# A pad of 64 bytes behind the weight buffers of a two-layer transformer kernel

## The chip, the cores and the metric

The kernel runs on one core of one Trainium2 chip. The time is that of one execution on the device in microseconds (us); three executions are given, and their median counts. One more execution was taken with the hardware profiler, and all rows shown here come from it.

## What is computed

The reference is a small hybrid transformer in fp32: 512 tokens, width 1024, two layers. Cut to its core:

```python
for layer in range(2):
    if layer == 0:    # attention with a forget gate, 16 heads of 64
        x = x + fox_mixer(rmsnorm(x, fox_norm), w_fox_in, b_fox_f, w_fox_out)
    else:             # latent attention, 16 heads, 128 + 64 rotary
        k_nope, k_rope, v = mla_shared_kv(x, kv_in_norm, w_dkv, kv_norm, w_uk, w_uv, cos, sin)
        x = x + mla_mixer(rmsnorm(x, mla_norm), w_dq, q_norm, w_uq, w_mla_out, k_nope, k_rope, v, cos, sin)
    x = x + conv_ffn(rmsnorm(x, ffn_norm[layer]), w_ffn_in[layer], conv_w[layer], conv_b[layer], w_ffn_out[layer])
return rmsnorm(x, final_norm)
```

## The kernel before

Activations are kept transposed: 128 features on the partitions, the 512 tokens along the row. Every fp32 number that goes through TensorE is split into a high and a low part, and a product is made of three matmuls: high weight by high activation, high by low, low by high. `mm3` (L82) issues them as L84, L85 and L86. For each matmul TensorE reads two operands from SBUF: the stationary one (here called the weight read, the first operand, LDWEIGHTS in the trace, 128 columns of 4 bytes on each partition) and the moving one (mostly 512 columns of 4 bytes). In `mm3` the stationary operand is a piece of a weight matrix and the moving one an activation. In two places it is the other way round: `mm_v` (L416 to L418) and `proj_v` (L687 to L689) hold the activation and stream the weights. The transposes of the attention (L227) hold a tile of the probabilities and stream the identity matrix `idf`.

`load_w` (L88) brings every weight: SyncE issues the DMA into a tile `raw`, ScalarE makes the high part `whi` (L105), VectorE or GpSimd the low part `wlo` (L106). There are three `raw` buffers and two each of `whi` and `wlo`, 4096 bytes a partition each.

The stages follow each other: the V projection (`mm_v`), then 16 heads of the first attention with the Q and K projections and part of the output projection filled in between, the first feed-forward block, the latent attention in the same manner, the second feed-forward block, and a tail that normalises and writes out in two halves. Order is program order on each engine.

Where a buffer lies within a partition follows from the order of the pools and the sizes of their tiles: pools lie one behind the other in the order in which they are opened, a tag's buffers one behind the other in the order in which tags first appear, and sizes are rounded up to 32 bytes. So there lie, in this order: `sp` (small things), `cp` (the residual `xT`, `idf`, `ones_r`, the scratch tiles `r2` and `R`), `wp` (`raw`, `whi`, `wlo`), `bp` (three buffers `big` of 32768 bytes, which hold the split activations), and the pool of the stage (`fx`, `ffn0`, `ml`, `ffn1`), with the probabilities, the split queries and keys, the third part of the feed-forward activations `act2` and so on. The buffers of `wp` come to 3 x 4096 + 2 x 4096 + 2 x 4096 = 28672 bytes, which is 112 x 256. All sizes in `cp`, `bp` and the stage pools add up to multiples of 256 too; where a small tile would break this it is made larger than what is used, as in

```python
        bfb = T(fp, [P, 64], F32, "bfb", 1)[:, :FH]
        rl = T(p_pool, [P, 16], F32, "rl", 2)[:, :NT]
            conv = T(fp, [P, 192], F32, "conv", 1)[:, :KF * 8]...
```

So every operand that TensorE reads in this kernel starts at the same place modulo 256 as every other one, with few exceptions. The one that matters here is the first third of `mm_v`, whose weight tile has two halves of 272 columns: the second, `w[0][:, 1, :]`, starts 272 x 4 = 1088 = 4 x 256 + 64 bytes into its buffer. The order of that stage is, for each of four pairs `kp`: 12 matmuls on the first half (kk = 0), then 12 on the second (kk = 1).

Of the kernel before, what the change touches and what calls it, by code (L numbers as in the profile page):

```python
# [7 lines left out]
F32 = mybir.dt.float32  # L8
# [7 lines left out]
P = 128  # L16
# [30 lines left out]
def tile_kernel(ctx, tc, xT_d, gains_d, bf_d, const_d, conv_d, wv_d, wq_d, wk_d, wfo_d,  # L47
                wdq_d, wdkv_d, wuqn_d, wuqr_d, wuk_d, wuv_d, wmo_d, wfi_d, wfu_d, out_d):
    nc = tc.nc
    v, a, g, pe = nc.vector, nc.scalar, nc.gpsimd, nc.tensor  # L50
# [4 lines left out]
    wp = ctx.enter_context(tc.tile_pool(name="wp", bufs=2))  # L55
# [2 lines left out]
    dp = ctx.enter_context(tc.tile_pool(name="dp", bufs=1, space=DRAM))  # L58

    cnt = [0]  # L60

    def T(pool, shape, dt, tag, bufs=None):
        cnt[0] += 1
        kw = {} if bufs is None else {"bufs": bufs}
        return pool.tile(shape, dt, tag=tag, name=f"{tag}_{cnt[0]}", **kw)
# [13 lines left out]
    def f(ap):  # L79
        return ap.bitcast(F32)  # L80
# [7 lines left out]
    def load_w(src, shape, gain=None, eng=None, into=None, pieces=1):  # L88

        n = 1  # L90
        for s in shape[1:]:
            n *= s
        raw = T(wp, [P, 1024], F32, "raw", 3)[:, :n]
        cuts = [slice(i * n // pieces, (i + 1) * n // pieces) for i in range(pieces)]
        for c in cuts:
            nc.sync.dma_start(raw[:, c], src[:, c])
        if gain is not None:
            k, c = gain
            r3 = raw.rearrange("p (k c) -> p k c", c=n // k)
            g.tensor_tensor(out=r3, in0=r3, in1=c.unsqueeze(2).to_broadcast([P, k, n // k]), op=ALU.mult)  # L100
        if into is None:
            into = T(wp, [P, 1024], F32R, "whi", 2), T(wp, [P, 1024], F32R, "wlo", 2)
        hi, lo = (t[:, :n] for t in into)
        for c in cuts:
            a.copy(hi[:, c], raw[:, c])  # L105
            (eng or v).tensor_tensor(out=lo[:, c], in0=raw[:, c], in1=f(hi[:, c]), op=ALU.subtract)  # L106
        names = " ".join(f"d{i}" for i in range(len(shape) - 1))
        kw = {f"d{i}": shape[i + 1] for i in range(len(shape) - 1)}
        pat = f"p ({names}) -> p {names}"
        return hi.rearrange(pat, **kw), lo.rearrange(pat, **kw)  # L110
# [168 lines left out]
    def ffn(layer, xs, squares, gbase):  # L279
        with tc.tile_pool(name=f"ffn{layer}", bufs=1, reuse_waits="tile") as fp:  # L280
# [21 lines left out]
            for j in range(KF):  # L302
                for b in range(2):
                    wh, wl = load_w(wfi_d[layer, j, b], [P, KD, P])
                    pt = acc()
                    for k in range(KD):
                        mm3(pt, (wh[:, k, :], wl[:, k, :]), parts(xs, k), k == 0, k == KD - 1)
                    rstd.after(lambda R, j=j, b=b, pt=pt: evacuate(j, b, pt, R))
# [3 lines left out]
            def load(d, c):  # L312
                k0, kn = chunks[c]
                return load_w(wfu_d[layer, d, :, k0 * P:(k0 + kn) * P], [P, kn, P])
# [76 lines left out]
    with tc.tile_pool(name="fx", bufs=1, reuse_waits="tile") as fp:  # L391
# [7 lines left out]
        def load_v(c, kp):  # L399
            if c == 2:  # L400
                nc.sync.dma_start(xT[:, 2 * kp, :], xT_d[2 * kp])
            w = load_w(wv_d[c][kp], [P, 2, VCH[c + 1] - VCH[c]], pieces=2 if (c, kp) == (2, 0) else 1)
            if c == 2:
                nc.sync.dma_start(xT[:, 2 * kp + 1, :], xT_d[2 * kp + 1])
            return w
# [475 lines left out]
```

## Time and profile before

| | us |
|---|---|
| three executions | 1430.11, 1433.37, 1434.18 |
| median | 1433.37 |
| the profiled execution | 1429.15 |
| its span, from the first to the last instruction | 1427.1 |
| TensorE busy | 1384.2 (97% of the span) |
| VectorE busy | 902.9 (63%) |
| ScalarE busy | 636.5 (45%) |
| GpSimd busy | 310.6 (22%) |
| mean granted TensorE clock | 0.983 of full speed |

The profiled execution lies 2.05 us above its span and 4.22 us (0.29%) below the median of the three. A matmul's recorded time runs into the next one's, since they are pipelined; what a matmul costs in a stream is the distance from its start to the start of the next.

### The profile page before, as it was taken

Reading aid. Unit: us, or ns where it says so; the run is one execution under the profiler, and the core shown is the slowest. Engines: PE = TensorE matmul, PEld = TensorE weight load, DVE = VectorE, ACT = ScalarE, POOL = GpSimd, SP = SyncE. Lnnn points to the kernel's source line nnn. Section 1 sums busy time; section 2 is a strip of 40 time slices with the busy share of each in tenths; the row PEclk is TensorE's granted clock in tenths of the full one; section 3 lists DMA queues with packets and bytes.
Section 4 is the critical chain, followed back from the end, with each engine's and each line's share of the span. In section 5 each row is a group of like instructions: output and inputs, shape, how many; then the busy total and the mean of one; then the engine's idle time right before and its main releaser. Section 6 shows DMA issues by size and latency. Waiting matters only on the chain.

```text
span 1427.1 us, 17362 instructions
## 1 busy us (share of the span) xinstructions
PE 1384.2 (97%) x6594; PEld 1162.8 (81%) x6594; DVE 902.9 (63%) x1495; ACT 636.5 (45%) x1103; POOL 310.6 (22%) x228
## 2 busy tenths in 40 slices
PE   7999999899999999999799999999999999999997
PEld 7888887788888888888678888888888888888886
DVE  6667786677776744445876666665557777774333
ACT  5588884254444432223454555543225444442111
POOL 4333322400000002154533333321310000000222
PEclk9999999999999999999999999999999999999998
DMA  5321112222323233332111111212232323323331
GB/s 178 102 76 61 51 51 68 89 96 96 103 90 104 89 92 97 106 105 80 50 49 48 59 49 52 61 54 89 89 104 89 104 91 101 98 94 93 96 97 69
DMA packets 41251, 120.22 MB, mean 84 GB/s; under 512 B 5552, under 2 KB 9952, under 8 KB 41168
## 3 DMA queue, kind: packets, MB, share of 16 engines
q1 hardware_dynamic: 39184, 117.00, 25.8%
q0 software_dynamic: 1840, 2.09, 0.6%
q8 instruction: 51, 0.84, 0.2%
q14 instruction: 32, 0.26, 0.1%
q10 hardware_dynamic: 144, 0.03, 0.0%
HBM read 116.74 MB, written 2.36 MB: 83 GB/s over the span
## 4 chain that ended last, share of the span: by engine, by line
PE 85%; DVE 8%; ACT 3%; issue 3%; DMA 1%; POOL 1%; SPq 0%; DVEq 0%; POOLq 0%; ACTq 0%
PE acc L84 24%; PE acc L86 23%; PE acc L85 23%; PE att L208 6%; DVE r L637 2%; PE acc L556 1%; PE att L227 1%; PE acc L709 1%; DVE r L638 1%; DVE ptl L231 1%; DVE big L190 1%; ACT whi L105 1%; DVE tr L667 1%; PE att L84 1%; PE att L86 1%
## 5 line engine op out<-in xcount | busy, mean ns | idle before, releaser
L86 PE MATMUL acc<-big,wlo 128*128 128x512 f32 (+1 forms) x1504 | 584.9, 389 | 7.5 <-POOL wlo L106 3.9
L84 PE MATMUL acc<-big,whi 128*128 128x512 f32 (+1 forms) x1504 | 587.5, 391 | 3.1 <-ACT big L189 2.2
L85 PE MATMUL acc<-big,whi 128*128 128x512 f32 (+1 forms) x1504 | 584.5, 389 | 0.3 <-DVE big L190 0.3
L105 ACT CAST whi<-raw 128x1024 fp32r<-128x1024 f32 (+4 forms) x243 | 229.3, 944 | 427.7 <-PE acc L85 267.5
L86 PEld LDWEIGHTS acc<-big,wlo 128*128 128x128 f32 x1504 | 283.8, 189 | 67.9 <-POOL wlo L106 5.8
L84 PEld LDWEIGHTS acc<-big,whi 128*128 128x128 f32 x1504 | 283.7, 189 | 61.0 <-ACT big L189 2.8
L85 PEld LDWEIGHTS acc<-big,whi 128*128 128x128 f32 x1504 | 283.8, 189 | 58.2 <-DVE big L190 0.6
L106 DVE TENSOR_TENSOR wlo<-raw,whi 128x1024 fp32r<-128x1024 f32 (+3 forms) x179 | 236.2, 1320 | 141.0 <-ACT whi L105 138.3
L142 POOL TENSOR_TENSOR r<-xT 128x512 f32<-128x512 f32 x28 | 31.4, 1124 | 735.9 <-DVE xT L254 414.5
L106 POOL TENSOR_TENSOR wlo<-raw,whi 128x768 fp32r<-128x768 f32 (+3 forms) x64 | 111.8, 1749 | 223.1 <-ACT whi L105 197.3
L294 DVE SCALAR_TENSOR_TENSOR c<-u,conv,c 128x510 f32<-128x510 f32 (+1 forms) x176 | 131.1, 747 | 3.5 <-ACT c L292 0.6
L289 DVE TENSOR_TENSOR u<-acc,R 128x512 f32<-128x512 f32 x88 | 60.3, 687 | 76.3 <-PE acc L86 76.3
L213 ACT ACTIVATE e<-e,nm 128x128 f32<-128x128 f32 (+3 forms) x128 | 71.3, 557 | 43.1 <-DVE nm L211 42.1
L146 POOL TENSOR_TENSOR r<-r,r 128x512 f32<-128x512 f32 x38 | 72.1, 1898 | 27.7 <-ACT r L140 21.0
L292 ACT ACTIVATE c<-u,conv 128x512 f32<-128x512 f32 x88 | 71.4, 813 | 3.1 <-DVE u L289 2.7
L298 ACT ACTIVATE sg<-c 128x512 f32<-128x512 f32 x44 | 27.8, 632 | 78.9 <-DVE c L294 78.8
L231 DVE TENSOR_TENSOR ptl<-att,pth 128x512 fp32r<-128x512 f32 (+3 forms) x128 | 55.4, 481 | 3.4 <-ACT pth L230 2.6
L186 ACT CAST big<-sg 128x512 fp32r<-128x512 f32 x32 | 19.9, 621 | 81.7 <-DVE sg L299 81.6
L230 ACT CAST pth<-att 128x512 fp32r<-128x512 f32 (+3 forms) x128 | 46.9, 435 | 4.8 <-PE att L227 4.3
L208 PE MATMUL att<-kn,tn 128*128 128x128 f32 (+2 forms) x192 | 47.7, 364 | 0.0
L217 DVE TENSOR_SCALAR e<-e,rl 128x128 f32<-128x128 f32 (+3 forms) x128 | 43.0, 399 | 1.1
L254 DVE TENSOR_TENSOR xT<-acc,xT 128x512 f32<-128x512 f32 x20 | 13.8, 691 | 42.5 <-PE acc L86 42.5
(180 smaller groups left out, 1563.8 us busy)
## 6 DMA issues: line engine op xcount, KB each, us to landing
raw<-in_wfi SPq DMA_DIRECT2D x88, 512.0 KB, 3.5
raw<-in_wfu SPq DMA_DIRECT2D x32, 512.0 KB, 3.5
raw<-in_wmo SPq DMA_DIRECT2D x16, 512.0 KB, 3.6
raw<-in_wfu SPq DMA_DIRECT2D x16, 384.0 KB, 3.1
raw<-in_wuqn SPq DMA_DIRECT2D x16, 384.0 KB, 3.0
raw<-in_wq SPq DMA_DIRECT2D x8, 512.0 KB, 3.5
raw<-in_wk SPq DMA_DIRECT2D x8, 512.0 KB, 3.4
raw<-in_wv SPq DMA_DIRECT2D x8, 384.0 KB, 3.1
```

The costliest lines, as they stand in the source:

```text
L84: pe.matmul(out, wh, xh, start=start, stop=False)
L85: pe.matmul(out, wh, xl, start=False, stop=False)
L86: pe.matmul(out, wl, xh, start=False, stop=stop)
L105: a.copy(hi[:, c], raw[:, c])
L106: (eng or v).tensor_tensor(out=lo[:, c], in0=raw[:, c], in1=f(hi[:, c]), op=ALU.subtract)
L146: (adder or g).tensor_tensor(out=self.sum, in0=self.sum, in1=sq, op=ALU.add)
L208: pe.matmul(s_ps[:, :n], lt, rt, start=(j == 0), stop=(j == len(mms) - 1))
L213: a.activation(e, e, AF.Exp, scale=-1.0, bias=nm[:, i:i + 1], accum_out=l[:, i:i + 1])
L231: v.tensor_tensor(out=lo, in0=pt[:, :w], in1=f(hi), op=ALU.subtract)
L289: v.tensor_tensor(out=u, in0=pt, in1=R, op=ALU.mult)
L292: a.activation(c, u, AF.Identity, scale=cw[:, 2:3], bias=cw[:, 3:4])
L294: v.scalar_tensor_tensor(out=c[:, s:], in0=u[:, :S - s], scalar=cw[:, 2 - s:3 - s], in1=c[:, s:], op0=ALU.mult, op1=ALU.add)
```

## The change

The first call of `load_w` that makes its own `whi` and `wlo` also makes a tile `pad` of 16 fp32 numbers, 64 bytes a partition, in the same pool `wp`, with one buffer, and VectorE sets it to zero. Nothing else uses it. As its tag appears last in `wp`, it lies behind `wlo`; `bp` and the pools of the stages lie 64 bytes further on than before, and `sp`, `cp`, `raw`, `whi` and `wlo` stay.

```diff
     cnt = [0]
+    pads = []
...
         if into is None:
             into = T(wp, [P, 1024], F32R, "whi", 2), T(wp, [P, 1024], F32R, "wlo", 2)
+            if not pads:
+                pads.append(T(wp, [P, 16], F32, "pad", 1))
+                v.memset(pads[0], 0.0)
         hi, lo = (t[:, :n] for t in into)
```

## Rows read from the trace of the kernel before

**Rows 1.** The page: engines' busy time, share of the span, instructions; then slices.

```profile
PE 1384.2 (97%) x6594; PEld 1162.8 (81%) x6594; DVE 902.9 (63%) x1495; ACT 636.5 (45%) x1103; POOL 310.6 (22%) x228
...
PEclk9999999999999999999999999999999999999998
```

**Rows 2.** The page: the chain that ended last, by engine.

```profile
PE 85%; DVE 8%; ACT 3%; issue 3%; DMA 1%; POOL 1%; SPq 0%; DVEq 0%; POOLq 0%; ACTq 0%
```

**Rows 3.** Groups by form, TensorE's weight loads: busy us, mean ns, idle before.

```profile
L85 PEld LDWEIGHTS acc<-big,whi 128*128 128x128 f32 x1504 | 283.8, 189 | 58.2 <-DVE big L190 0.6 <-DVE big L187 0.2 <-DVE big L642 0.2
...
L227 PEld LDWEIGHTS att<-idf,e 128*128 128x128 f32 x320 | 36.8, 140 | 3.6
...
L85 PEld LDWEIGHTS acc<-act,whi 128*128 128x128 f32 x102 | 19.2, 188 | 3.5
...
L688 PEld LDWEIGHTS acc<-wlo,big 128*128 128x128 f32 x64 | 12.2, 191 | 0.3
...
L85 PEld LDWEIGHTS att<-big,whi 128*128 128x128 f32 x16 | 3.0, 189 | 0.5
```

**Rows 4.** TensorE's matmuls in order, second feed-forward block, 512 columns: start, duration.

```profile
1299.78 0.39 PE L86 MATMUL acc<-big,wlo 128*128 128x512 f32 x1
...
1302.50 0.39 PE L86 MATMUL acc<-big,wlo 128*128 128x512 f32 x1
```

**Rows 5.** The same in the tail, 256 columns.

```profile
1404.40 0.28 PE L84 MATMUL acc<-big,whi 128*128 128x256 f32 x1
...
1405.84 0.28 PE L84 MATMUL acc<-big,whi 128*128 128x256 f32 x1
```

**Rows 6.** The same in `mm_v`, 272 columns, every twelfth; at 23.45 the next third begins.

```profile
17.40 0.29 PE L416 MATMUL acc<-whi,big 128*128 128x272 f32 x1
...
18.91 0.29 PE L416 MATMUL acc<-whi,big 128*128 128x272 f32 x1
...
20.43 0.29 PE L416 MATMUL acc<-whi,big 128*128 128x272 f32 x1
...
21.94 0.29 PE L416 MATMUL acc<-whi,big 128*128 128x272 f32 x1
...
23.45 0.33 PE L416 MATMUL acc<-whi,big 128*128 128x384 f32 x1
```

**Rows 7.** Groups by form in 20.428 to 21.939 us (kk = 0): busy us, mean ns, idle before.

```profile
L417 PE MATMUL att<-wlo,big 128*128 128x272 f32 x3 | 0.9, 289 | 0.0
L418 PE MATMUL att<-whi,big 128*128 128x272 f32 x3 | 0.9, 287 | 0.0
L416 PE MATMUL acc<-whi,big 128*128 128x272 f32 x2 | 0.6, 291 | 0.0
L417 PE MATMUL acc<-wlo,big 128*128 128x272 f32 x2 | 0.6, 290 | 0.0
L418 PE MATMUL acc<-whi,big 128*128 128x272 f32 x2 | 0.6, 287 | 0.0
L416 PE MATMUL att<-whi,big 128*128 128x272 f32 x2 | 0.6, 287 | 0.0
```

**Rows 8.** The same in 21.939 to 23.454 us (kk = 1); its L417 att row equals Rows 7's.

```profile
L418 PE MATMUL att<-whi,big 128*128 128x272 f32 x3 | 0.9, 289 | 0.0
...
L417 PE MATMUL acc<-wlo,big 128*128 128x272 f32 x2 | 0.6, 289 | 0.0
L418 PE MATMUL acc<-whi,big 128*128 128x272 f32 x2 | 0.6, 289 | 0.0
L416 PE MATMUL att<-whi,big 128*128 128x272 f32 x2 | 0.6, 289 | 0.0
L416 PE MATMUL acc<-whi,big 128*128 128x272 f32 x2 | 0.6, 286 | 0.0
```

**Rows 9.** The timeline of the first 6 us: VectorE, and the first matmul.

```profile
0.82 0.06 DVE L124 MEMSET small<- 128x2 f32 x1 [0.82 <-PEq L870]
0.87 0.17 DVE L126 MEMSET ones_r<- 128x128 f32 x1
0.99 0.06 DVE L127 MEMSET small<- 128x4 f32 x1
1.09 0.48 DVE L476 MEMSET pth<- 16x512 f32 x1
...
4.65 0.75 DVE L190 SCALAR_TENSOR_TENSOR big<-xT,gains,big 128x512 fp32r<-128x512 f32 x1 [3.07 <-ACT big L189]
...
4.98 0.82 PE L416 MATMUL acc<-whi,big 128*128 128x272 f32 x2 [4.98 <-ACT whi L105]
```

**Rows 10.** The page's DMA issues: KB each, median us from issue to landing.

```profile
xT<-in_xT SPq DMA_DIRECT2D x8, 256.0 KB, 6.3
...
out_xT<-o SPq DMA_DIRECT2D x8, 256.0 KB, 2.1
```

## The prediction

> **What bounds the kernel now.** I read the page first. TensorE is busy 1384.2 of 1427.1 us and its clock is granted in full in nearly every slice [rows 1]; the chain that ended last is TensorE for 85% of the span [rows 2]. So this kernel is a long stream of matmuls, and an edit counts if it changes what one matmul costs, or what happens in the few places where TensorE isn't the last to end.
>
> What a matmul costs in the stream is the distance between starts. With 512 columns twelve of them take 1302.50 - 1299.78 = 2.72 us, 226.7 ns each [rows 4]; with 256 columns twelve take 1405.84 - 1404.40 = 1.44 us, 120.0 ns each [rows 5]. The difference is 106.7 ns for 256 columns, 0.417 ns a column, which is one column a cycle at the granted 2.4 GHz. What is left over is 226.7 - 512 x 0.417 = 13.3 ns, in both shapes: a fixed piece for each pair of weight load and matmul. The weight load itself takes 189 ns and lies beside the matmul before it [rows 3]. The question of this change is whether those 13.3 ns, or more, hang on where the two operands lie relative to each other.
>
> **The change, part by part.**
>
> *Which matmuls get another distance.* The weights stay and everything in `bp` and the stage pools moves by 64 bytes, so an operand pair changes its distance if one of it is in `whi`, `wlo` or `cp` and the other isn't. Those of `mm3` with `whi` and `wlo` are three times (1504 + 102 + 16) [rows 3], where one row stands for each of the three lines, = 4866; their moving operand comes to lie 64 past the weights modulo 256. In 320 transposes, 192 matmuls of `proj_v` (three times 64) [rows 3] and the 288 of `mm_v` (by the code 3 thirds x 4 pairs x 24) the weight read moves and the stream doesn't: the distance is 64 the other way, except for the second halves of the 272-column third, where it falls from 64 to nothing. The rest (the scores, the products with the probabilities, the pieces of the output projection whose weights lie in the stage pool) have both operands behind the pad and keep their distance.
>
> *What the distance of 64 costs or gives.* The trace of before has a sample of it. In the third of `mm_v` that is 272 columns wide the halves kk = 0 read both operands at the same place modulo 256, and the halves kk = 1 stream their weights from 64 further on: the sign and size that the 4866 get. All else is equal: same engine, width, activations, clock. The starts are 17.40, 18.91, 20.43, 21.94, 23.45 [rows 6]: kk = 0 takes 1.51 and 1.51 us, kk = 1 takes 1.52 and 1.51. Over 24 matmuls each that is 125.8 against 126.3 ns, a difference of +0.4 ns where one rounded hundredth is 0.4. The recorded durations are finer: weighted by their counts the groups of kk = 0 come to 288.4 ns [rows 7], those of kk = 1 to 288.6 [rows 7, 8], +0.1 ns. Nor does the fixed piece shrink at a distance of 64: 126.3 - 272 x 0.417 = 12.9 ns are left, against 13.3 in the long stream at distance zero. I take 0 (a difference of 0.1 ns is less than the view resolves); the ends are 0.8 ns a matmul for the worse (two hundredths on 24) and 0.4 ns for the better (one hundredth), which is 4866 x 0.83 = +4.1 us and 4866 x 0.42 = -2.0 us.
>
> There is a reason in the rows why a start distance should matter little. A weight load goes through 512 bytes a partition in 189 ns, 2.7 bytes a ns; the stream goes through 4 bytes in 0.417 ns, 9.6 bytes a ns. In one load they drift apart by 189 x 6.9 = 1300 bytes, five times 256, so every distance modulo 256 comes up wherever they start. That is worked out from durations; the trace shows no single read.
>
> The Trainium skill (TensorE: Matmul & The Clock Gate, step-by-step part of Part 2) speaks against the change too: by it TensorE has two independent read ports, one for the streamed operand and one for the weight load, so that a load takes nothing from the running matmul. By that the term is nothing at any distance, and the sample above agrees.
>
> *The 800 whose weight read moves.* By the same +0.8 or -0.4 ns they are worth +0.7 or -0.3 us; I take 0. The transposes' loads, 140 ns each [rows 3], are the ones nearest to setting a pace, and even 5 ns on each of 320 would be 1.6 us.
>
> *The memset.* One VectorE instruction of 16 columns. The nearest rows are the memsets of 2 and of 4 columns, 0.06 us each, and that of 128, 0.17 [rows 9]. It is issued ahead of the memset of L476 at 1.09; VectorE then waits 3.07 us for ScalarE, until 4.65 [rows 9]. That wait hides it. Without the cover it would cost 0.06 to 0.17 us, once.
>
> *Transfers.* The loads of weights land in `raw`, which doesn't move. The output tiles `o` do, and the last of the eight transfers ends the kernel, 2.1 us from issue to landing [rows 10]. No row shows a transfer of this size from 64 past such a boundary; between nothing and a landing as slow as that of the input tiles of the same size, 6.3 us under the rush of the start [rows 10], that is 0 to +4.2 us. I take 0, as the bytes are the same and the tail's queue is nearly empty.
>
> The Trainium skill (DMA: Bandwidth & Descriptors, How a descriptor splits into AXI transactions) has a price: a descriptor that starts off a 256-byte boundary fetches from the boundary below. For 1024-byte rows that makes 34 beats of 32, an estimate of 0.13 us on 2.1; no run here shows it.
>
> *What doesn't change.* The waits stay as they are, and the memset is the one instruction added. Nothing else waits for `pad`. VectorE, ScalarE and GpSimd read and write the same shapes, some with one operand 64 bytes further on; their share is 63% at most [rows 1], so a few per cent on one of them would lie behind TensorE.
>
> **Sum.** 0 (4866) + 0 (800) + 0 (memset) + 0 (transfers) = 0. On the profiled execution that is 1429.15 us. It was 4.22 us below the median of the three, and the median is what a new median is set against, so I forecast 1433.4.
>
> **The rivals.**
>
> *A, faster: the fixed piece is a clash of the two reads and 64 bytes apart they don't meet.* For it: 13.3 ns is 32 cycles, and a load is 32 times 16 bytes, so that one lost cycle for each 16 bytes would come out exactly. Against it: 12.9 ns of it are still there in the sample at distance 64 [rows 6]; but that sample has 24 matmuls, of one width, with the roles of weight and activation exchanged. If all of it went: 4866 x 13.3 = 64.7 us, 1368.7. If a tenth went, 6.5 us, 1426.9. The Trainium skill (TensorE: Matmul & The Clock Gate, the section on 56 against 53.3 ns) gives a fixed cost of about 2.5 ns for back-to-back matmuls; by it 10.8 ns could go, an estimate of 52.6 us and 1380.8. These rows don't bear it out at either distance. Chance 0.12: 0.04 for most of the piece, 0.08 for a part of it.
>
> *B, slower: the reads meet more often at 64, and the cost goes with the columns streamed.* The sample's upper end is 0.83 ns for 272 columns; for 512 it would be 1.57 ns, and 4866 x 1.57 = +7.6 us, 1441.0. For it: the one row of kk = 1 that is a hundredth longer [rows 6]. Against it: the durations differ by 0.1 ns [rows 7, 8]. It decides from 4.3 / 4866 = 0.9 ns a matmul. Chance 0.10.
>
> *C, the pad does not part the streams.* If it lay elsewhere than behind `wlo`, or everything moved together, the distance would stay. The time is then the forecast's, 1433.4, and it is part of the forecast's chance; the stretch of 272 columns would tell it apart.
>
> **How the numbers follow.** 0.3% is 4.3 us, about what a measurement of this kernel can tell from no change: the three executions alone spread over 4.1 us. The forecast (with C) has 0.78, A 0.12, B 0.10. These are also the chances of the same, faster and slower. The range reaches up to B's 1441.0, which takes in the upper end of the 4866 and that of the transfers; downward to 1427.0, which is about the forecast less the 2.3 us of both groups and the 4.2 us by which the profiled execution was below the median (1426.9), and takes in a tenth of A. What it leaves out is the greater part of A and anything worse than B, 1 to 2 in 10.
>
> **What would show it.** If I am right, the matmuls of 512 columns start 226.7 ns apart and those of 256 columns 120.0; loads of `whi` and `wlo` stay at 189 ns; a memset of `pad` lies near 1.1 us on VectorE and the first matmul still starts at 4.98 [rows 9]; TensorE's busy time stays within 4 us of 1384.2. In `mm_v` the halves exchange roles (kk = 1 at no distance, kk = 0 at 64 the other way) and all stay at 126 ns. A distance between starts that differs by 1 ns or more in the long stream makes the prediction wrong, in the direction that it moves; a time that moves while 226.7 stays would mean that I overlooked a cost on another engine or in the tail.

## The result, and the profile after

The changed kernel is slower by half a per cent: 1437.38 us, the median of eight executions (1434.85 to 1439.37), against 1429.82 us for eight of the kernel before (1426.96 to 1434.18). The ratio is 1.0051 with a 95% interval of 1.0035 to 1.0067, which is +5.0 to +9.6 us. The profiled execution took 1437.95 us, 1.95 us more than its span, and 8.80 us more than the profiled execution of before.

These lines are from the page of the changed kernel: the span, the engines' busy time, and then the groups of `mm3` with their busy time in us and the mean duration of one matmul in ns. One line was added above `mm3`, so its L84, L85 and L86 of before are now L85, L86 and L87; lines behind `load_w` moved by four:

```profile
span 1436.0 us, 17363 instructions
...
PE 1394.7 (97%) x6594; PEld 1165.1 (81%) x6594; DVE 904.4 (63%) x1496; ACT 634.8 (44%) x1103; POOL 310.7 (22%) x228
...
L85 PE MATMUL acc<-big,whi 128*128 128x512 f32 (+1 forms) x1504 | 593.2, 395 | 3.1 <-ACT big L193 2.2
L87 PE MATMUL acc<-big,wlo 128*128 128x512 f32 (+1 forms) x1504 | 589.0, 392 | 7.1 <-POOL wlo L110 3.6
L86 PE MATMUL acc<-big,whi 128*128 128x512 f32 (+1 forms) x1504 | 584.7, 389 | 0.2 <-DVE big L194 0.2
```

and these are the same three groups on the page of the kernel before:

```profile
L86 PE MATMUL acc<-big,wlo 128*128 128x512 f32 (+1 forms) x1504 | 584.9, 389 | 7.5 <-POOL wlo L106 3.9
L84 PE MATMUL acc<-big,whi 128*128 128x512 f32 (+1 forms) x1504 | 587.5, 391 | 3.1 <-ACT big L189 2.2
L85 PE MATMUL acc<-big,whi 128*128 128x512 f32 (+1 forms) x1504 | 584.5, 389 | 0.3 <-DVE big L190 0.3
```

TensorE is busy 10.5 us longer than before [rows 1], the span is 8.9 us longer, and the other engines moved by 2 us or less. The same number of matmuls takes longer, while the time that TensorE waits ahead of these three groups is no longer than it was.

How much longer is plain in the long stream of the second feed-forward block. This view is the groups by form of the changed kernel in the stretch 1250 to 1350 us (busy us, mean ns):

```profile
L85 PE MATMUL acc<-big,whi 128*128 128x512 f32 x128 | 50.5, 394 | 0.0
L87 PE MATMUL acc<-big,wlo 128*128 128x512 f32 x128 | 50.2, 392 | 0.0
L86 PE MATMUL acc<-big,whi 128*128 128x512 f32 x128 | 49.7, 388 | 0.0
```

and this the same stretch of the kernel before, in which all three take 389 ns:

```profile
L84 PE MATMUL acc<-big,whi 128*128 128x512 f32 x128 | 49.8, 389 | 0.0
L85 PE MATMUL acc<-big,whi 128*128 128x512 f32 x128 | 49.8, 389 | 0.0
L86 PE MATMUL acc<-big,wlo 128*128 128x512 f32 x128 | 49.8, 389 | 0.0
```

The three lines have drifted apart by +5, +3 and -1 ns. The starts say the same: in the timeline of the changed kernel the 15 matmuls from one L86 to another take 1303.39 - 1299.95 = 3.44 us, 229.3 ns each, where 226.7 stood before [rows 4].

```profile
1299.95 0.39 PE L86 MATMUL acc<-big,whi 128*128 128x512 f32 x1
...
1303.39 0.39 PE L86 MATMUL acc<-big,whi 128*128 128x512 f32 x1
```

In the tail, with 256 columns, it goes the other way. The timeline of the changed kernel there: 36 matmuls take 1414.26 - 1410.02 = 4.24 us, 117.8 ns each against 120.0 [rows 5].

```profile
1410.02 0.28 PE L85 MATMUL acc<-big,whi 128*128 128x256 f32 x1
...
1414.26 0.28 PE L85 MATMUL acc<-big,whi 128*128 128x256 f32 x1
```

The memset of the pad is where it was expected, ahead of VectorE's long wait. It takes 0.07 us, and the wait of 3.09 us for ScalarE covers it. VectorE's timeline of the changed kernel at the start:

```profile
1.00 0.07 DVE L106 MEMSET pad<- 128x16 f32 x1
...
4.69 0.75 DVE L194 SCALAR_TENSOR_TENSOR big<-xT,gains,big 128x512 fp32r<-128x512 f32 x1 [3.09 <-ACT big L193]
```

In `mm_v` the last four halves of the 272-column third start at 18.45, 19.93, 21.44 and 22.93 us, and the next third at 24.43. So the two halves kk = 0, now 64 apart the other way, take 1.48 and 1.49 us (123.3 and 124.2 ns a matmul), and the two halves kk = 1, now at no distance, 1.51 and 1.50 us (125.8 and 125.0 ns). The prediction had 126 ns for all; the halves that changed to 64 the other way became a little cheaper, and none became dearer.

### The profile page after: what moved, and what is told of

The parts are those of the page before. It is cut to its first block, busy times and chain, and to the rows that moved or that the text cites. A ratio compares the mean times of both kernels' runs of the same rounds, so it can differ in the third digit from the quotient of the medians.

```text
span 1436.0 us, 17363 instructions
## 1 busy us (share of the span) xinstructions
PE 1394.7 (97%) x6594; PEld 1165.1 (81%) x6594; DVE 904.4 (63%) x1496; ACT 634.8 (44%) x1103; POOL 310.7 (22%) x228
## 4 chain that ended last, share of the span: by engine, by line
PE 85%; DVE 8%; issue 3%; ACT 3%; POOL 1%; DMA 1%; SPq 0%; DVEq 0%; ACTq 0%; POOLq 0%
PE acc L85 24%; PE acc L87 23%; PE acc L86 23%; PE att L212 6%; DVE r L641 2%; PE acc L713 1%; PE acc L560 1%; PE att L231 1%; DVE r L642 1%; DVE big L194 1%; DVE ptl L235 1%; ACT whi L109 1%; DVE wlo L110 1%; PE att L85 1%; PE att L87 1%
## 5 line engine op out<-in xcount | busy, mean ns | idle before, releaser
L85 PE MATMUL acc<-big,whi 128*128 128x512 f32 (+1 forms) x1504 | 593.2, 395 | 3.1 <-ACT big L193 2.2
L87 PE MATMUL acc<-big,wlo 128*128 128x512 f32 (+1 forms) x1504 | 589.0, 392 | 7.1 <-POOL wlo L110 3.6
L86 PE MATMUL acc<-big,whi 128*128 128x512 f32 (+1 forms) x1504 | 584.7, 389 | 0.2 <-DVE big L194 0.2
L87 PEld LDWEIGHTS acc<-big,wlo 128*128 128x128 f32 x1504 | 283.6, 189 | 72.6 <-POOL wlo L110 5.3
L86 PEld LDWEIGHTS acc<-big,whi 128*128 128x128 f32 x1504 | 283.6, 189 | 61.1 <-DVE big L194 0.6
L85 PEld LDWEIGHTS acc<-big,whi 128*128 128x128 f32 x1504 | 284.3, 189 | 59.4 <-ACT big L193 2.6
```

The lines of the kernel that those rows point to most:

```text
L85: pe.matmul(out, wh, xh, start=start, stop=False)
L86: pe.matmul(out, wh, xl, start=False, stop=False)
L87: pe.matmul(out, wl, xh, start=False, stop=stop)
```

## The experiments

Three theories were on the table. D: the distance between the place of the weight read and that of the stream, modulo 256, sets what a matmul costs. P: it is the place of the stream alone. E: it is something else in the edit, the added instruction or tiles of the other engines that lie differently.

**e1_streams.** A bench with TensorE alone. Each activation tile is larger by 64 bytes and more, and a slice of it makes the distance:

```diff
+    for d in DIST:
+        x = mp.tile([P, 1024 + 64], F32R, name=f"x{d}B")
+        o = d // 4
+        hi, lo = x[:, o:o + S], x[:, o + S:o + 2 * S]
...
+        for j, (w_, x_) in enumerate(seq):
+            pe.matmul(pt[:, :n], w_, x_[:, :n], start=(j == 0), stop=(j == len(seq) - 1))
```

> A bench of TensorE alone: it leaves the whole network out, writes a copy of an input instead of the result, and runs the three matmuls of mm3 over one weight tile and activations that lie at 14 distances behind the weights (0 to 240 bytes modulo 256), 48 matmuls each with 512 and with 256 columns, and a few with 384 or with one of the three matmuls alone. All other engines rest. Theory D (the distance between the weight read and the stream sets the cost of a matmul): at distance 0 starts are 226.7 ns apart with 512 columns and 120.0 with 256; at 64 they are 229.2 on average with 512 (231.6, 225.8, 229.3 by line) and 117.5 with 256; other distances give other values. Theory P (where the stream itself starts modulo 256 sets it): here the weights start at 128 modulo 256, so the 226.7 ns would be found at distance 128, where the stream starts at 0, and not at distance 0. Theory E (something else in the edit: the added instruction, or other engines reading and writing tiles 64 bytes further on): 226.7 and 120.0 at every distance, as nothing else runs.

Each bench was executed once. This is the timeline of the bench, the first matmul of some of the groups; a tile's name tells its distance, and each group has 48 matmuls (from 197.07 on with 256 columns):

```profile
40.87 0.39 PE L141 MATMUL acc<-x0B,whi 128*128 128x512 f32 x1
...
51.75 0.40 PE L141 MATMUL acc<-x4B,whi 128*128 128x512 f32 x1
...
96.69 0.39 PE L141 MATMUL acc<-x64B,whi 128*128 128x512 f32 x1
...
107.67 0.40 PE L141 MATMUL acc<-x80B,whi 128*128 128x512 f32 x1
...
141.08 0.39 PE L141 MATMUL acc<-x128B,whi 128*128 128x512 f32 x1
...
152.23 0.39 PE L141 MATMUL acc<-x160B,whi 128*128 128x512 f32 x1
...
185.88 0.39 PE L141 MATMUL acc<-x240B,whi 128*128 128x512 f32 x1
...
197.07 0.28 PE L141 MATMUL acc<-x0B,whi 128*128 128x256 f32 x1
...
202.83 0.29 PE L141 MATMUL acc<-x4B,whi 128*128 128x256 f32 x1
...
225.62 0.28 PE L141 MATMUL acc<-x64B,whi 128*128 128x256 f32 x1
...
231.27 0.28 PE L141 MATMUL acc<-x80B,whi 128*128 128x256 f32 x1
```

With 512 columns a matmul costs (51.75 - 40.87) / 48 = 226.7 ns at distance 0, (107.67 - 96.69) / 48 = 228.8 at 64 and (152.23 - 141.08) / 48 = 232.3 at 128. With 256 columns it is 5.76 / 48 = 120.0 at 0 and 5.65 / 48 = 117.7 at 64. Both kernels' numbers come out with the other engines at rest (but for a copy of two columns behind each group), so E falls for the matmuls. By the order and the sizes of the pools the weights lie at 128 modulo 256 here, and at 0 in the kernel before; distance 0 still has the 226.7, so P falls too.

The pattern of three unequal matmuls at distance 64 came back even where all three read the same stream and the same kind of weights (the group at 64 on the high part alone, 229.2 ns on average, settles into steps of 226, 229 and 232 ns in turn). So it doesn't come from the three lines of `mm3`.

**e2_ahead64.** The pad and its memset ahead of the weight buffers:

```diff
     def load_w(src, shape, gain=None, eng=None, into=None, pieces=1):
+        if not pads:
+            pads.append(T(wp, [P, 16], F32, "pad", 1))
+            v.memset(pads[0], 0.0)
```

> The same pad and the same memset, but ahead of the weight buffers in their pool: weights and activations all move by 64 bytes, so mm3, mm_v and proj_v keep distance 0; only the transposes have the distance that the change gives them. Theory D: 226.7 ns apart with 512 columns, the time of before (ratio 0.998 to 1.002). Theory P: streams start at 64 modulo 256, 229.2 ns and about 1.005. Theory E: the added instruction and the shift of the activations against xT and the scratch tiles are there, about 1.005.

It took 1429.72 us, ratio 1.0004 (0.9995 to 1.0013). Its groups by form in 1250 to 1350 us are back at one value:

```profile
L87 PE MATMUL acc<-big,wlo 128*128 128x512 f32 x127 | 49.4, 389 | 0.0
L85 PE MATMUL acc<-big,whi 128*128 128x512 f32 x126 | 49.0, 389 | 0.0
L86 PE MATMUL acc<-big,whi 128*128 128x512 f32 x126 | 49.0, 389 | 0.0
```

The activations lie 64 further on here too, against `xT` and the scratch tiles as in the changed kernel, and so does the output in the tail; the memset is there. Only the distance between weights and activations is that of before, and the whole loss is gone. P falls here again: every stream of `mm3` starts 64 further on, at the time of before. The transposes, which have the changed kernel's distance here, cost nothing that shows.

**e3_pad128 and e4_pad192.** The change with a larger pad, `[P, 32]` and `[P, 48]` in place of `[P, 16]`:

```diff
-                pads.append(T(wp, [P, 16], F32, "pad", 1))
+                pads.append(T(wp, [P, 32], F32, "pad", 1))    # e3; [P, 48] in e4
```

> The pad of the change made 128 bytes. Theory D: a third value of the spacing with 512 columns, not 226.7 and not 229.2 on average; within 213.3 (one column a cycle and nothing else) and 240. Theory P: as with 64, or worse the further from 0; the time at or above the changed kernel's. Theory E: the changed kernel's time, 1.005.

> The pad of the change made 192 bytes: mm3 gets the distance that mm_v and proj_v have in the changed kernel (64 the other way), where 256 columns took 114 ns against 120 before and 384 about 175 against 173.5. Theory D: 256 columns at 114 ns in the tail; for 512 columns a fixed gain per load would be 221 ns and a ratio of 0.98, but the 384 columns make 226 to 230 and 1.000 to 1.007 likelier. Theory P: as the changed kernel or worse. Theory E: 1.005.

The pad of 128 took 1451.78 us, ratio 1.0148 (1.0131 to 1.0166), the one of 192 took 1453.29 us, 1.0163 (1.015 to 1.0176). One line of each in 1250 to 1350 us, groups by form, first e3:

```profile
L85 PE MATMUL acc<-big,whi 128*128 128x512 f32 x131 | 51.7, 395 | 0.0
```

then e4:

```profile
L85 PE MATMUL acc<-big,whi 128*128 128x512 f32 x131 | 51.8, 396 | 0.0
```

All three lines of each are at 395 to 396 ns, +6 to +7 on 389, which fits the bench's 232.3 ns at 128 (+5.6) and 233.3 at 192 (+6.6). With 256 columns the pad of 192 was a gain, as theory D had it: in the tail of e4 36 matmuls take 1427.91 - 1423.83 = 4.08 us, 113.3 ns each. So the pad's size matters and the loss isn't that of having a pad. My guess for 192 (226 to 230 ns, at most 1.007) was too low: I had carried over what 256 and 384 columns did at that distance, the same mistake as in the prediction.

**e5_all_distances.** The bench with 64 distances in steps of 4 bytes, 24 matmuls each.

> The bench of TensorE alone again, with every distance from 0 to 252 bytes in steps of 4, 24 matmuls each with 512 and then with 256 columns, all on the high part (it leaves the network out and writes a copy of an input). Theory D: 226.7 ns at distance 0 with 512 columns, 228.9 at 64, 232.3 at 128, 233.3 at 192, and at no distance less than 226.7 by more than one ns, since the first bench found none among its 14; with 256 columns between 113.3 (at 112) and 123 (at 4). Rival L (distance 0 is only a lucky one among several, and a better one lies between the 14): some distance is at 220 ns or below with 512 columns, and a pad of that size would make the kernel faster by 4734 x 6 ns = 28 us.

Among the 64 the least with 512 columns is 226.7 ns, at 0 and, within half a ns, at a few others (28, 60, 156, 236, 240 and 252); most lie at 230 to 235, and the worst, at 240, are 20, 132, 196 and 244. Three of them as the timeline shows the groups' first matmuls, 20, 240 and 244:

```profile
58.47 0.40 PE L133 MATMUL acc<-x20B,whi 128*128 128x512 f32 x1
...
64.23 0.40 PE L133 MATMUL acc<-x24B,whi 128*128 128x512 f32 x1
...
366.18 0.39 PE L133 MATMUL acc<-x240B,whi 128*128 128x512 f32 x1
...
371.62 0.40 PE L133 MATMUL acc<-x244B,whi 128*128 128x512 f32 x1
...
377.38 0.40 PE L133 MATMUL acc<-x248B,whi 128*128 128x512 f32 x1
```

At 20 and at 244 a matmul costs 5.76 / 24 = 240.0 ns, at 240 it is 5.44 / 24 = 226.7. No distance beats 0 for the shape of which the kernel is made, so rival L falls. With 256 columns 0 lies in the middle (119.6) and two distances, 16 and 144, reach 113.3.

Not every number of e1 comes back. At 240 e1 has (197.07 - 185.88) / 48 = 233.1 ns where e5 has 226.7, and with 256 columns at 16 it has 116.9 where e5 has 113.3. By the order of the pools the operands lie at the same places modulo 256 in both benches. They differ in what is streamed (three pairs there, the high part alone here), in the length of the groups and in what ran just before, so these places alone don't set the cost; no run takes the rest apart. With 512 columns at 0, 64, 128 and 192, the distances of the kernels, the two benches agree within about 1 ns.

**e6_weight_columns.** The bench with narrower weight loads, `wh[:, j % KD, :m]` for m of 128, 64 and 32.

> The bench with weight loads of 128, 64 and 32 columns at distances 0, 4, 64, 128 and 192, 48 matmuls of 512 columns each (it leaves the network out). Theory W (each weight load takes turns from the stream, so the loss goes with what the load reads): over the 213.3 ns of 512 columns, 13.3 ns at distance 0 with 128 columns become about 7 with 64 and 3 to 4 with 32, and the differences between distances shrink in the same way. Rival F (a fixed piece for the change of weights, and only the rest is a clash): 13.3 ns at distance 0 at every width of the load, and the other distances come down to it.

Both theories missed. The starts of the groups at distance 0 and the group behind it, 48 matmuls each, 64 columns of weights and then 32:

```profile
85.45 0.40 PE L133 MATMUL acc<-x0B,whi 128*64 128x512 f32 x1
...
96.50 0.39 PE L133 MATMUL acc<-x4B,whi 128*64 128x512 f32 x1
...
140.82 0.39 PE L133 MATMUL acc<-x0B,whi 128*32 128x512 f32 x1
...
151.92 0.40 PE L133 MATMUL acc<-x4B,whi 128*32 128x512 f32 x1
```

With 64 columns a matmul costs 11.05 / 48 = 230.2 ns, with 32 it is 11.10 / 48 = 231.3, though a load of 32 columns takes 109 ns where one of 128 takes 188:

```profile
L133 PEld LDWEIGHTS acc<-x0B,whi 128*32 128x32 f32 x48 | 5.2, 109 | 5.9
```

At distance 0 a quarter of the weights cost the stream not less but 4.6 ns more. At 128 it went the other way (232.1 ns with 128 columns of weights, 229.2 with 64, 230.4 with 32). So the loss doesn't go with what the load reads, nor is it a fixed piece for changing weights.

**e7_projv112.** The kernel before, with `proj_v` at the distance that was best for 256 columns in the first bench:

```diff
-            wh, wl = load_w(wuv_d[j], [P, KL, 2 * MV], eng=g)
+            into = [T(wp, [P, 1024], F32R, t, 2)[:, 28:] for t in ("whi", "wlo")]
+            wh, wl = load_w(wuv_d[j], [P, KL, 2 * MV], eng=g, into=into)
```

> The kernel before with one edit: proj_v puts its weights 112 bytes into the weight tiles, so that its 192 matmuls of 256 columns get the distance at which the first bench had 113.3 ns instead of 120.0, while mm3 stays at distance 0. Theory D: the three lines of proj_v drop to 113 to 114 ns, the long stream stays at 226.7, and the time falls by at most 192 x 6.7 = 1.3 us, 0.999, which the times can hardly tell. If the distance doesn't carry over from the bench: 120 ns and 1.000.

It took 1429.16 us, ratio 1.0004 (0.9989 to 1.0018): no difference. Its matmuls did become shorter, a median of 278 ns against 283 for the first of the three lines, but 5 ns on 192 of them is under 1 us, which the times can't tell. The 113 ns of the bench come only after a while: these are the first, the eleventh and the eighteenth matmul of one call in e7's timeline.

```profile
729.48 0.28 PE L688 MATMUL acc<-whi,big 128*128 128x256 f32 x1
...
730.65 0.28 PE L689 MATMUL acc<-wlo,big 128*128 128x256 f32 x1
...
731.44 0.28 PE L690 MATMUL acc<-whi,big 128*128 128x256 f32 x1
```

The first ten steps take 1.17 us, 117 ns each, and the next seven 0.79 us, 113 ns each. So what a distance gives in a long stream isn't what it gives in a stretch of a dozen matmuls.

**e8_pairs.** The bench with one distance made in several ways, to see whether the distance modulo 256 is all that counts:

```diff
+    PAIRS = {64: ((0, 64), (192, 0), (64, 128), (0, 320)), 0: ((64, 64), (128, 128), (20, 20), (0, 256)),
+             20: ((0, 20), (236, 0), (20, 40), (0, 276))}
```

> The bench with 512 columns, in which a distance is made in four ways each, 48 matmuls for each pair (it leaves the network out). Written as weights at, stream at: distance 64 as (0, 64), (192, 0), (64, 128), (0, 320); distance 0 as (64, 64), (128, 128), (20, 20), (0, 256); distance 20 as (0, 20), (236, 0), (20, 40), (0, 276). Theory D (the distance modulo 256 alone): 229 ns in the first four, 226.7 in the second, 240 in the third. Rival M (the distance counts, but not modulo 256): the last of each four and the second, where the stream lies 192 or 236 below, differ from the rest. Rival A (the stream's own place modulo 64 or 256 counts as well): the pairs of one distance differ among themselves.

The starts of the groups, 48 matmuls each; the names tell where weights and stream lie:

```profile
45.95 0.39 PE L140 MATMUL acc<-w0x64X,w0x64W 128*128 128x512 f32 x1
...
56.94 0.40 PE L140 MATMUL acc<-w192x0X,w192x0W 128*128 128x512 f32 x1
...
67.95 0.39 PE L140 MATMUL acc<-w64x128X,w64x128W 128*128 128x512 f32 x1
...
78.94 0.39 PE L140 MATMUL acc<-w0x320X,w0x320W 128*128 128x512 f32 x1
...
89.93 0.39 PE L140 MATMUL acc<-w64x64X,w64x64W 128*128 128x512 f32 x1
...
100.82 0.39 PE L140 MATMUL acc<-w128x128X,w128x128W 128*128 128x512 f32 x1
...
111.75 0.40 PE L140 MATMUL acc<-w20x20X,w20x20W 128*128 128x512 f32 x1
...
123.03 0.40 PE L140 MATMUL acc<-w0x256X,w0x256W 128*128 128x512 f32 x1
...
133.93 0.39 PE L140 MATMUL acc<-w0x20X,w0x20W 128*128 128x512 f32 x1
...
145.25 0.40 PE L140 MATMUL acc<-w236x0X,w236x0W 128*128 128x512 f32 x1
```

The four ways to 64 take 10.99, 11.01, 10.99 and 10.99 us, 229 ns a matmul each; no distance, made as (64, 64), (128, 128) and (0, 256), takes 10.89, 10.93 and 10.90 us, 227 to 228. So with 512 columns D holds for these distances at places that are multiples of 64, and modulo 256. Off such places it doesn't: 20 and 20, at no distance, take (123.03 - 111.75) / 48 = 235.0 ns, and the distance of 20 takes 11.32 / 48 = 235.8 ns as (0, 20), but 231.7 as (236, 0) and 233.1 as (20, 40). There the pairs of one distance differ among themselves, as rival A had it. That the place itself is the reason is not shown: e5 had 240.0 ns for the distance of 20 from weights at the same place modulo 256 as in (0, 20). Every buffer of this kernel that the change concerns starts at a multiple of 64.

## Why the prediction was right in its bounds and wrong in its likeliest case

The time lies in the range, between the forecast of 1433.4 and its upper end of 1441.0, but what came isn't the case that I thought likeliest. A time within 0.3% of before had 0.78; the measured +0.35 to +0.67% is rival B's, to which I gave 0.10. B's +7.6 us is close to the measured difference by luck: its size was taken from the edge of a rounded row, and its mechanism, a cost that goes with the columns streamed, is not what the bench shows (at 64: -2.3 ns with 256 columns, 0 with 384, +2.1 with 512).

*What bounds the kernel.* Right. The loss is in TensorE's stream, and little of it was hidden: TensorE is busy 10.5 us longer, and the span grew by 8.9.

*The 4866 matmuls at 64: taken as 0.* This is the step that failed. The page has the three groups of `mm3` at 593.2 + 589.0 + 584.7 us now, and had 587.5 + 584.5 + 584.9 before: +10.0 us on 4512 matmuls, 2.2 ns each on average. I had allowed at most 0.8 ns. The sample in the trace was real, and it showed what it showed for 272 columns; carrying it over to 512 was the error. What a distance costs depends on the number of columns, and changes its sign: at 64 the bench of e1 has +2.1 ns for 512 columns, nothing for 384 (173.3 at 0 and at 64) and -2.3 for 256. The sample also had the roles of weights and activations exchanged, and it came in stretches of 12 matmuls, where e7 needs about ten to come to its settled cost. No run here takes these two apart from the width. I also counted all 4866 as 512 columns wide; 132 of them, in the tail, have 256 and gained.

*The argument from drift* (that the two reads pass through every distance anyway, so that the start can't matter) fell with e1 and e8. Where they start does decide, in steps as small as 4 bytes (226.7 ns at 0, 236.7 at 4 in e5).

*The fixed piece of 13.3 ns*, which I read off two widths, isn't fixed. It is at distance 0, where 256, 384 and 512 columns all lose 13.3; at other distances the remainder was anything from 6.7 ns (256 columns at their best) to 26.7 (512 columns at 20).

*The rule of two independent read ports* (the Trainium skill, TensorE: Matmul & The Clock Gate, step-by-step part of Part 2) made the term nothing at any distance. The runs differ: 226.7, 228.8 and 232.3 ns at 0, 64 and 128, with the other engines at rest. The measurement decides; the weight load and the stream aren't independent of each other's place.

*The 800 whose weight read moves.* Near enough to 0 in the sum. The 192 of `proj_v` gained 0.7 us: by the groups by form they take 18.8 + 17.8 + 17.8 us in the changed kernel, and took 18.9 + 18.1 + 18.1 before. The transposes stayed as they were (40.6 us in both, and in e2).

*Memset and transfers.* Right: e2 has the memset and the moved output tiles, and the time of before.

*Rival A*, that 64 bytes would part two reads which clash at distance 0, was wrong in its sign for 512 columns. *Rival C* is excluded: the pad did part them.

*The base.* I set the forecast on the median of three executions; with eight it is 3.55 us lower. Measured from there the loss is 7.56 us, the very edge of what the range allowed upward (7.6 us); that the time lies well inside the range owes to the base being too high.

What stays open is how the two reads get in each other's way. e6 excludes that the loss simply grows with what the load reads. Three things point to a matmul's cost also hanging on how the ones before it went: the three unequal matmuls in a row with one stream and one kind of weights, the slow start in e7, and the two costs at one distance in e1 and e5. No run here goes further.

## What to carry to other kernels

A kernel that streams matmuls without a gap pays for where its operands lie, a few ns each time; over the 4866 matmuls of `mm3` that came to 0.5% here with a pad of 64 bytes and to 1.5 and 1.6% with 128 and 192. Sweep the distance between weights and activations in a bench of TensorE alone, with the very number of columns, the order of operands and the lengths of stretch that the kernel uses, before padding anything. A number read off one shape isn't a number for another, however alike they are; the natural sample in a trace settles the case only for its own width. When a pad is tried, try it on the other side too (both operands moved together): that one run tells the distance from everything else that the pad brings.

## What the runs showed of the hardware

With 512 columns and 128 columns of weights a matmul in an unbroken stream at the full clock cost between 226.7 and 240.0 ns with the other engines at rest, as the places of its two operands changed; with 256 columns between 113.3 and 123. With 512 columns and places that are multiples of 64 bytes, distances of 0 and 64 modulo 256 cost the same wherever the two operands lay (227 to 228 and 229 ns); off such places (20 and 20: 235.0 ns) they didn't. The places modulo 256 don't set the cost alone: at a distance of 240 one bench had 233.1 ns and another 226.7. Of 64 distances none was better than 0 for 512 columns, and a narrower weight load (32 columns, 109 ns instead of 188) made a matmul at distance 0 dearer by 4.6 ns, and at 128 cheaper by 1.7.
